# A one-core decoder block: from the planner's instruction order to an order written as a table

## The chip, the cores and the metric

The kernel runs on one core of one Trainium2 chip. The metric is the device time of one execution in microseconds, as the median of the runs. The core has a tensor engine (PE, with its weight loads shown apart as PEld), a vector engine (DVE), a scalar engine (ACT), GpSimd (POOL) and a sync engine (SP) that issues most transfers. Each of them takes its own instructions strictly in the order in which the program lists them, and waits on semaphores for what the others produce. This document is about nothing but that order.

## What is computed

One layer of a hybrid decoder block on 512 tokens of width 1024, in fp32:

```python
h = h + 0.5 * swiglu(rmsnorm(h, norm_ffn1), w1, w3, w2)          # FFN 1, hidden width 2816
z = rmsnorm(h, norm_mix) @ w_in
q, kc, vc, ksl, vsl, kw, vw, g, u = split(z)
o_nsa = nsa_attention(rope(q), ...)     # compressed + selected + window branches, 8 heads of 64
o_s5  = s5_mixer(u, ...)                # 32 groups of 16 channels, 64 states, a scan over time
h = h + concat([o_nsa, o_s5]) @ w_out
h = h + 0.5 * swiglu(rmsnorm(h, norm_ffn2), ...)                 # FFN 2
gate = sigmoid(rmsnorm(h, norm_ple) @ w_ple_gate)
h = h + gate * (p @ w_ple)
return rmsnorm(h, norm_final)
```

## The kernel before

**Number format.** Most products are made of three tensor-engine products (`mm3`, line 157, with `mm` at line 131): each operand is split into a high part and a low part in the fp32r format, and high x high, high x low and low x high are added up in PSUM. A unit of 128x1024 weights comes in by one transfer (`load_unit`, line 103, tile `raw`), ACT casts it to `hi` (line 152), DVE subtracts to get `lo` (line 154). Plain fp32 operands are used only in small products: the S5 scan, the compression branch (`raw` against `cs`, `cosr`, `sinr`), the S5 output gate (`yt`), the row sums of the norms (`ones`) and transposes against `ident`.

**Stages, in order.** FFN 1 in four chunks (`ffn`, line 345; from block 7 of 22 on with a scheme of seven half products, `up_fast`, line 403, whose weights are summed by two accumulating transfers from POOL, lines 362 and 368), with the constants of the S5 scan computed beside it (`s5_constants`). Then the mixer: projections with rotation (`proj`, `rotary`, `kq`), the S5 input `u8`, the S5 scan in eight chunks (`s5_in`, line 904: a product with `si` into bank C, four DVE steps, four scans, one multiply that gives `z`; `s5_out`: products with `so` into bank D; `s5_back`: transposes of `ysb`, copied to `yt`), the scores of four query blocks (`scores`, line 1136: two products and a mask into bank B or C, a row maximum on DVE at line 1169, an exponential on ACT at line 863), the compression branch (`cmp_all`), the S5 output gate (`glu`: two ACT and two DVE steps on each of four `yt`, lines 864 to 871, then products with `yt`), the attention values (`values`, line 1233: products into bank C, two exponentials `e` and `eh`, a subtraction `el` on DVE at line 1264, two products with `VL` into bank D) and the output projection in two halves (`out_half`, the first half is meant to fill gaps between the values). Then a norm, FFN 2, the gate in two column halves, the last norm and the output.

**What sets the order.** The source issues 8,878 instructions and tile-pool marks in the order of its Python loops. The tile framework then takes them and plans, with a model of the durations, an order for each engine in which it keeps data dependencies and the reuse of buffers. The source holds it back in some places: `keep_in_program_order` (called `pinned`) and `issue_after` (in `split`, `combine`, `aside`, `late`, `act`) say that one instruction may not come before another. Weight loads are issued by SP while `more` is set (inside both FFNs) and otherwise by ACT (line 141).

The prediction speaks of source positions: the place of an instruction in that list of 8,878, counted from 0. Those used are

| position | instruction |
|---|---|
| 3543 to 3546 | first S5 product with `si`, chunk 0 |
| 3547 / 4268 | first DVE step of S5 chunk 0 / last DVE step on the fourth `yt` |
| 3887, 3888 | casts of `QA`, `QB` for the second four heads of query block 2 (lines 1149, 1150) |
| 3605 to 3703 | first six exponentials of the scores of query block 3 (line 863) |
| 4160, 4267 | copy of the fourth `yt` out of PSUM (line 947), its Tanh (line 863) |
| 4314 | first product with `yt` |
| 2069, 2088 | cast of `ah` (line 370) and copy of `zx` into bank B (line 399) of one block of FFN 1 |

## Time and profile before

| | us |
|---|---|
| median of 3 runs | 1095.88 |
| lowest, highest | 1093.8, 1096.82 |
| the profiled execution's own time | 1096.0 |
| its span, first to last instruction | 1094.2 |
| PE busy | 1042.1 |
| DVE busy | 794.0 |
| ACT busy | 516.8 |
| POOL busy | 92.7 |

The profile's busy time of PE is a union of matmul records whose ends are modelled, so that a matmul record is longer than the time to the next matmul. Where matmuls run without waiting, the time per matmul is read from the chain that ended last: a run of so many matmuls in so many microseconds. PEclk is the share of the tensor engine's full clock that was granted.

### The profile page before, as it was taken

Reading aid. Unit: us, or ns where it says so; the run is one execution under the profiler, and the core shown is the slowest. Engines: PE = TensorE matmul, PEld = TensorE weight load, DVE = VectorE, ACT = ScalarE, POOL = GpSimd, SP = SyncE. Lnnn points to the kernel's source line nnn. Section 1 sums busy time; section 2 is a strip of 40 time slices with the busy share of each in tenths; the row PEclk is TensorE's granted clock in tenths of the full one; section 3 lists DMA queues with packets and bytes.
Section 4 is the critical chain, followed back from the end, with each engine's and each line's share of the span. In section 5 each row is a group of like instructions: output and inputs, shape, how many; then the busy total and the mean of one; then the engine's idle time right before and its main releaser. Section 6 shows DMA issues by size and latency. Waiting matters only on the chain.

```text
span 1094.2 us, 16835 instructions
## 1 busy us (share of the span) xinstructions
PE 1042.1 (95%) x6446; PEld 897.5 (82%) x6446; DVE 794.0 (73%) x1339; ACT 516.8 (47%) x911; POOL 92.7 (8%) x118
## 2 busy tenths in 40 slices
PE   6999999998999999979799999999999999999996
PEld 4887999798889788767377668799899899898895
DVE  6999786786787766777468887976477557566766
ACT  5334255344435423346647875555255245255541
POOL 5000010000000200010000001011010101000000
PEclk9999999999999999989899999999999999999998
DMA  9334366786657737773621026256365635535302
GB/s 284 137 99 112 81 166 171 192 200 153 166 130 187 234 97 226 216 218 111 187 68 40 0 97 173 77 146 176 84 144 142 177 73 143 171 96 153 111 8 77
DMA packets 86625, 151.14 MB, mean 138 GB/s; under 512 B 27648, under 2 KB 47104, under 8 KB 86544
## 3 DMA queue, kind: packets, MB, share of 16 engines
q1 hardware_dynamic: 66352, 98.11, 29.5%
q0 software_dynamic: 13152, 29.66, 13.7%
q10 hardware_dynamic: 7040, 22.29, 6.5%
q8 instruction: 50, 0.82, 0.3%
q14 instruction: 31, 0.25, 0.1%
HBM read 123.27 MB, written 17.83 MB: 129 GB/s over the span
## 4 chain that ended last, share of the span: by engine, by line
PE 62%; ACT 4%; issue 3%; DVE 3%; DMA 3%; ACTq 0%; SPq 0%; POOLq 0%; POOL 0%; DVEq 0%
PE ps_A L131 18%; PE ps_C L131 18%; PE ps_B L131 17%; PE ps_D L131 10%; DMA qf<-qd 2%; ACT e L863 1%; ACT eh L863 1%; ACT ps_B L863 1%; DMA raw<-in_wpack 1%; DVE el L1264 0%; DVE lo L154 0%; ACT hi L152 0%; DMA qd<-r 0%; ACT QA L1149 0%; ACT pt L1270 0%
## 5 line engine op out<-in xcount | busy, mean ns | idle before, releaser
L152 ACT CAST hi<-raw 128x1024 fp32r<-128x1024 f32 (+2 forms) x201 | 206.0, 1041 | 245.8 <-PE ps_C L131 103.5
L154 DVE TENSOR_TENSOR lo<-raw,hi 128x1024 fp32r<-128x1024 f32 (+2 forms) x201 | 240.0, 1218 | 70.8 <-ACT hi L152 66.4
L131 PE MATMUL ps_C<-hq,hi 128*128 128x512 f32 x704 | 218.0, 392 | 3.9 <-ACT hq L352 2.3
L131 PEld LDWEIGHTS ps_C<-hq,hi 128*128 128x128 f32 x704 | 130.4, 188 | 32.9 <-ACT hq L352 3.2
L131 PE MATMUL ps_A<-xh,hi 128*128 128x256 f32 (+1 forms) x456 | 141.0, 311 | 7.4 <-ACT xh L175 6.3
L131 PE MATMUL ps_A<-xl,hi 128*128 128x256 f32 (+1 forms) x456 | 141.2, 312 | 3.1 <-DVE xl L176 2.1
L131 PE MATMUL ps_A<-xh,lo 128*128 128x256 f32 (+1 forms) x456 | 140.9, 310 | 1.7 <-DVE lo L154 1.7
L131 PE MATMUL ps_C<-hq,lo 128*128 128x512 f32 x352 | 136.2, 390 | 0.0
L131 PEld LDWEIGHTS ps_A<-xh,hi 128*128 128x128 f32 x456 | 86.4, 190 | 12.7 <-ACT xh L175 6.2
L131 PEld LDWEIGHTS ps_A<-xl,hi 128*128 128x128 f32 x456 | 86.2, 190 | 11.6 <-DVE xl L176 4.7
L131 PEld LDWEIGHTS ps_A<-xh,lo 128*128 128x128 f32 x456 | 86.4, 190 | 6.2 <-DVE lo L154 1.9
L131 PE MATMUL ps_B<-sh,hi 128*128 128x256 f32 x280 | 79.1, 283 | 2.7 <-ACT ps_B L399 2.7
L131 PE MATMUL ps_B<-sh,lo 128*128 128x256 f32 x280 | 78.8, 281 | 0.7 <-DVE lo L154 0.7
L131 PE MATMUL ps_B<-sl,hi 128*128 128x256 f32 x280 | 78.9, 282 | 0.0
L131 PEld LDWEIGHTS ps_C<-hq,lo 128*128 128x128 f32 x352 | 66.1, 188 | 13.6
L362 POOL DMA_DIRECT2D raw<-in_wpack x35 | 30.4, 869 | 483.7 <-DVE h L1127 168.3
L488 DVE SCALAR_TENSOR_TENSOR h<-ps_C,h 128x512 f32<-128x512 f32 x64 | 43.9, 689 | 36.8 <-PE ps_C L131 36.4
L131 PE MATMUL ps_D<-sh,hi 128*128 128x256 f32 x220 | 61.7, 283 | 0.4 <-ACT hi L152 0.4
L131 PE MATMUL ps_D<-sh,lo 128*128 128x256 f32 x220 | 61.7, 281 | 0.0
L131 PE MATMUL ps_D<-sl,hi 128*128 128x256 f32 x220 | 61.3, 281 | 0.0
L131 PE MATMUL ps_B<-xh,hi 128*128 128x512 f32 (+1 forms) x164 | 57.9, 353 | 0.9 <-ACT hi L152 0.9
L131 PE MATMUL ps_B<-xh,lo 128*128 128x512 f32 (+1 forms) x160 | 56.0, 350 | 0.8 <-DVE lo L154 0.8
(402 smaller groups left out, 2327.4 us busy)
## 6 DMA issues: line engine op xcount, KB each, us to landing
raw<-in_wpack SPq DMA_DIRECT2D x132, 512.0 KB, 4.3
raw<-in_wpack ACTq DMA_DIRECT2D x40, 512.0 KB, 4.2
raw<-in_wpack POOLq DMA_DIRECT2D x35, 256.0 KB, 4.2
raw<-raw POOLq DMA_DIRECT2D x35, 256.0 KB, 3.4
so<-s5o POOLq DMA_DIRECT2D x8, 768.0 KB, 5.9
si<-s5i POOLq DMA_DIRECT2D x8, 512.0 KB, 5.6
h<-in_xT SPq DMA_DIRECT2D x8, 256.0 KB, 5.5
s5i<-fs SPq DMA_DIRECT2D x4, 512.0 KB, 4.6
```

Of the source, the lines that this page charges most:

```text
L131: return PE.matmul(o, lhsT, rhs, start=start, stop=stop, **kw)
L152: S.copy(hi[:, c], raw[:, c])
L154: V.tensor_tensor(lo[:, c], raw[:, c], hi[:, c].bitcast(F32), OP.subtract)
L362: nc.gpsimd.dma_start(a0[:, 1], src[:, 0:512], accum_op=OP.add)
L488: mark = V.scalar_tensor_tensor(h[:, m, :], o, 0.5, h[:, m, :], OP.mult, OP.add)
L863: S.activation(*args, **kw)
```

## The change

It takes all the holds out (`pinned`, `issue_after`, `aside`'s mark, `late`, `act` and the table of the activation set) and lets every weight load be issued by SP (43 loads of the mixer, of the row embedding and of the gate go from ACT's queue to SP's). No arithmetic, no tile and no loop is changed. In their place stand two tables and a function that is called when the source has issued everything:

```diff
-            load_unit(i, q or (nc.sync if more else nc.scalar))
+            load_unit(i, nc.sync)
...
-                with tc.issue_after(self.last.ins):
-                    for i in range(2):
-                        V.tensor_tensor(t[:, 2 * i:2 * i + 2], a(i), b(i), op)
+                for i in range(2):
+                    V.tensor_tensor(t[:, 2 * i:2 * i + 2], a(i), b(i), op)
...
-        def act(*args, **kw):
-            with tc.issue_after(table[0].ins):
-                S.activation(*args, **kw)
...
-        table.append(tc.keep_in_program_order(S.preload_act_table_set("exp_and_others")))
+        S.preload_act_table_set("exp_and_others")
...
+ENGINE_ORDER = {
+    "PE": (
+        "65:42 31:3 -34:3 3:4 -7:3 28:12 -27 26:30 23:6 -29:3 26:42 26:45 15:3 -18:3 15:18 3:3 -6:3 3:21 65:18 "
...
+    "DVE": (
+        "611 -2 -582 11 -15 -3 5 11 -9 -3 5 -3 26 70 263 232 -233 -264 263:4 6 -7 6 -7:5 2:2 -298 297:7 -303 309 "
...
+    "ACT": (
+        "4 46 -24 11 -15 -3 24 -20 17 -7 -11 1 1 1 14 9 -9 1 1 74 -74 74 64 2 -76 2 54 87 -86 87 -17 -8 79 -70 "
...
+    "SP": (
+        "8 -4 1 -2 2 2 -3:2 1:3 184 193:2 2 -3:2 390:2 -774 770 -585 587 -6 3 -6 -512 2 56 2 109 2 83 2 114 27 "
...
+TILE_ORDER = (
+    "51>792 395>1091 604>948 2341>2356 3185>3260 3186>3261 3227>4160 3281>3594 3468>3731 3532>3556 3533>3562 "
...
+def impose(tc):
+    traced = list(tc.nc.cur_bb.bb.instructions)
+    follow = mybir.DependencyInfo(mybir.DependencyClass.NoSync, mybir.DependencyReason.DATA)
+    for moves in ENGINE_ORDER.values():
+        at, before = 0, None
+        for move in moves.split():
+            step, _, count = move.partition(":")
+            at += int(step)
+            for _ in range(int(count or 1)):
+                if before is not None:
+                    tc.add_manual_dep(traced[at], before.name, follow, reason="order")
+                before = traced[at]
+                at += 1
+    for pair in TILE_ORDER.split():
+        a, b = map(int, pair.split(">"))
+        tc.add_manual_dep(traced[b], traced[a].name, follow, reason="order of tiles")
...
         block_kernel(tc, aps, out)
+        impose(tc)
```

An entry `65:42` says: go 65 places on in the source's list and take 42 instructions in a row; the next entry's step counts from the place behind them, and may be negative. Read in this way the tables name every instruction of its engine once: 6,202 products for PE, 1,339 instructions for DVE, 850 for ACT (843 operations and 7 transfers), 114 for POOL and 333 transfers for SP. Each is made to follow the one in front of it on its engine, so the planner is left no choice. TILE_ORDER's 50 pairs say which of two instructions that share a buffer comes first.

Set side by side with the planner's order, about a third of PE's instructions stand elsewhere relative to the rest (1,996 of 6,202 are outside the longest common sequence; 557 of DVE's 1,339 and 309 of ACT's 850). The large moves are in the mixer:

- The first S5 product (position 3543) comes 123 products later on PE: the 48 products of the compression branch's projections, 51 of the value projection's and eight score groups of three go ahead of it.
- The scores' exponentials 3605 to 3703 come before the casts 3887 and 3888 on ACT; before, they stood behind them.
- All 16 products with `yt` stand in one run; the S5 gate's ACT steps stand close behind the copies of `yt`.
- Of the 192 products of `out_half`'s two calls (96 in each), 15 stand ahead of the first product with `VL`, 48 between the first and the last of them and 129 behind; before it was 96, 2 and 94.
- Neighbours on PE of which one is plain fp32 and the other is not: 93 places, 119 before.

In FFN 1, FFN 2 and the gate the order differs by swaps of groups of three (one `mm3`) between neighbouring runs.

## The prediction

> **What bounds the kernel now.** I read the page first, then the busy time by stretches, then who waited for whom, then the chain of waits around the longest waits. The page:

> ```profile
> PE 1042.1 (95%) x6446; PEld 897.5 (82%) x6446; DVE 794.0 (73%) x1339; ACT 516.8 (47%) x911; POOL 92.7 (8%) x118
> PE 62%; ACT 4%; issue 3%; DVE 3%; DMA 3%; ACTq 0%; SPq 0%; POOLq 0%; POOL 0%; DVEq 0%
> ```

> The tensor engine carries the chain. An order can win only where PE waits or runs slowly, so I ask in which stretches that is. Stretches of the run, with PE's, DVE's and ACT's busy time and PE's granted clock:

> ```profile
> 0.00:25.00 25.00, 15.66 (x59) 10.98 (x60) 16.92 (x15) 15.42 (x23) 13.35 (x16) 1.00 0.90 281
> ...
> 240.00:300.00 60.00, 55.60 (x386) 51.83 (x386) 42.48 (x73) 25.83 (x44) 6.96 (x8) 0.97 0.68 170
> 300.00:440.00 140.00, 137.81 (x764) 119.15 (x763) 99.40 (x154) 55.35 (x80) 12.49 (x22) 1.00 0.62 175
> ...
> 440.00:480.00 40.00, 32.78 (x220) 26.13 (x219) 30.67 (x66) 13.90 (x29) 3.81 (x7) 0.89 0.82 239
> 520.00:560.00 40.00, 33.06 (x155) 18.63 (x152) 19.55 (x35) 22.60 (x48) 0.00 (x0) 0.87 0.47 146
> 552.10:648.20 96.10, 92.37 (x459) 66.90 (x458) 80.41 (x170) 70.92 (x175) 0.00 (x0) 1.00 0.13 39
> 700.00:1000.00 300.00, 300.00 (x2122) 281.95 (x2121) 192.15 (x249) 136.74 (x220) 32.02 (x37) 1.00 0.51 131
> 1000.00:1060.00 60.00, 55.90 (x355) 49.46 (x354) 43.58 (x76) 29.24 (x47) 1.04 (x1) 1.00 0.28 89
> ```

> FFN 2 (700 to 1000) has nothing to give: PE is busy in 300.00 of 300.00 us. PE is idle 4.4 us in 240 to 300 and 2.2 in 300 to 440 (FFN 1), 7.2 in 440 to 480 and 6.9 in 520 to 560 (mixer), 3.7 in the attention (552 to 648) and 4.1 around the gate's start. What the longest waits are for:

> ```profile
> PE ps_B L131 <- ACT ps_B L863: 7.4, 4, 5.9
> PE ps_A L131 <- ACT xh L175: 6.3, 1, 6.3
> PE ps_A L131 <- DVE yt L871: 5.8, 1, 5.8
> PE ps_B L131 <- ACT ps_B L399: 2.7, 1, 2.7
> ```

> The second is the head of the kernel, before any data is there. The other three are mine to explain.

> **The wait for the scores (5.87 us).** The chain and ACT's timeline there:

> ```profile
> 461.45 11.19 DMA qf<-qd
> ...
> 474.15 1.35 PE ps_B L131 x3
> ```

> ```profile
> 472.67 0.63 ACT L1149 ACTIVATE QA<-qf 128x512 fp32r<-128x512 f32 x1 [0.65 <-DMA qf<-qd]
> 473.32 0.66 ACT L863 ACTIVATE ps_B<-ps_B,nmax 128x512 f32<-128x512 f32 x1
> ```

> PE's timeline of the same three products later on:

> ```profile
> 493.51 0.39 PE L131 MATMUL ps_B<-KA,QA 128*128 128x512 f32 x1
> ...
> 494.01 0.37 PE L131 MATMUL ps_A<-hi,xl 128*128 128x280 f32 x1
> ```

> The casts of query block 2 (positions 3888 and 3887) stand on ACT ahead of an exponential that has nothing to do with them. They wait for a transfer of 11.19 us, the exponential waits behind them, and PE waits for the bank that the exponential frees. In the table the first six exponentials of block 3 stand ahead of both casts, so this wait goes. So does the slow stretch behind it: three products took 1.35 us where the same three take 0.50 (493.51 to 494.01). Gain 5.87 + 0.85 = 6.7. What is late next is the exponentials themselves, with two buffers of bank B; I count that below.

> **The wait for the fourth yt (5.84 us).** ACT, DVE and PE:

> ```profile
> 524.32 0.58 ACT L947 COPY yt<-ps_D 128x512 f32<-128x512 f32 x1 [0.30 <-PE ps_D L942]
> ...
> 529.70 0.61 ACT L863 ACTIVATE gt<-yt 128x512 f32<-128x512 f32 x1
> ...
> 536.13 0.61 ACT L863 ACTIVATE gt<-gt 128x512 f32<-128x512 f32 x1
> ```

> ```profile
> 537.73 2.08 PE L131 MATMUL ps_A<-yt,raw 128*128 128x512 f32 x2 [5.84 <-DVE yt L871]
> ```

> ```profile
> 540.23 8.07 PE ps_A L131 x16
> ...
> 549.01 3.20 PE ps_A L131 x7
> ```

> Between the copy and the Tanh ACT does casts that are needed later: 11.8 us for a chain of four steps of about 0.6 us. In the table ten ACT instructions, some 6 us, lie between copy and Tanh, and PE has as cover the compression branch's last products, 32 small score products, two score groups and the first three products with yt (two records each, 0.46 us a record by the last row: 3.20 / 7): about 7 us. The chain is about 9 with its DVE steps and hops, so about 2 us of wait stay (an estimate from these rows). Gain: 5.84, and the slow products behind it, 2.08 - 2 x 0.46 = 1.2 for the first and 8.07 - 16 x 0.46 = 0.7 for the next: 7.7 less 2, so 5.7; I write 6.

> Here the clock enters. The row is this: after a wait of only 2.7 us at 264 PE is slow for a while.

> ```profile
> 265.08 1.75 PE ps_B L131 x10
> ...
> 278.50 1.19 PE ps_B L131 x10
> ```

> Ten products take 1.75 us in place of 1.19. So by the row the 2 us that stay could cost up to as much again, and the sum would be 1071 in place of 1069. [...]

> **Other waits in the mixer.** 7.2 + 6.9 us idle less the two waits leaves 2.4; I take 1.5 off, with 0 and 2.4 as bounds.

> **Plain fp32 products in runs.** A change of kind costs a product's start:

> ```profile
> 494.74 0.29 PE L131 MATMUL ps_A<-lo,xh 128*128 128x280 f32 x1
> 494.87 0.29 PE L131 MATMUL ps_A<-hi,xl 128*128 128x280 f32 x1
> 495.09 0.44 PE L131 MATMUL ps_D<-so,u 128*64 128x128 f32 x4
> 495.46 0.40 PE L131 MATMUL ps_A<-hi,xh 128*128 128x280 f32 x1
> 495.69 0.78 PE L131 MATMUL ps_C<-u,si 128*128 128x64 f32 x6
> ```

> 0.13 us from one to the next of a kind, 0.22 and 0.23 into plain fp32: 0.1 a change. The table has 93 changes, 119 before: 26 x 0.1 = 2.6 (bounds 0 and 5, if one costs 0.2).

> **Attention.** Before, half of out_half's products ran ahead of the values and next to none between them; the stretch's second half is then full on the other engines:

> ```profile
> 560.00:600.00 40.00, 39.20 (x214) 31.23 (x213) 32.85 (x66) 26.10 (x76) 0.00 (x0) 1.00 0.18 53
> 600.00:640.00 40.00, 38.17 (x166) 25.21 (x165) 36.18 (x81) 35.63 (x81) 0.00 (x0) 1.00 0.04 14
> ```

> PE looks busy in both, but runs 166 products in the second where it runs 214 in the first. The table starts the values earlier and puts 48 of those products between them, so that ACT's 70.92 us of the whole 96.10 are spread. If ACT got to 79% of the stretch in place of 74, it would be 90 long: gain 6. Bounds: 10 (ACT at 82%) and -3 (129 products now stand behind the last value, which nobody needs to cover).

> **FFN 1.** 4.4 + 2.2 idle, and the slow products. The wait at 264 has its cause on ACT: the cast of ah (2069) waits for an accumulating transfer and the copy that PE needs (2088) stands behind it. In the table it still does, so I take only part: 4, bounds 7 and -4 (swaps of threes make new waits like it).

> **What I cost at nothing.** Head: the table casts a later slice first (four ACT steps of 0.6 to 0.7 us more ahead of the first product, 1.5 us), and the five waits of 0.7 us for single slices go; 0, within 1.5. FFN 2 can only lose: 0, bound 6. The norm and the gate's start: row sums now stand right behind the last product of FFN 2 and wait for them, but the later wait for the norm goes; 0, within 2. The 43 loads:

> ```profile
> raw<-in_wpack SPq DMA_DIRECT2D x132, 512.0 KB, 4.3
> raw<-in_wpack ACTq DMA_DIRECT2D x40, 512.0 KB, 4.2
> ```

> ```profile
> 513.30 0.33 ACTq L111 DMA_DIRECT2D raw<-in_wpack  x1
> ```

> They land as fast from either queue, and 43 x 0.33 = 14 us of issuing leave ACT where ACT is not last; 0. On SP they now stand in line with the copies of q, k, kc and u, which wait for their producers, and every later load waits with them: bound 4. The end is as it was: the last row sums, the eight multiplies and the output have nothing beside them.

> **The sum.** 6.7 + 6 + 1.5 + 2.6 + 6 + 4 = 26.8 off the profiled execution's 1096.0 (span 1094.2) gives 1069.2; the median of the runs shown, 1095.88, is 0.1 below that execution, so 1069.

> **The rivals.**

> *The waits nearly all go.* All best bounds: 6.7 + 7.7 + 2.4 + 5 + 10 + 7 + 3.5 (head and gate) = 42.3, so 1054. For it: every order is fixed, and only real dependencies are left. Against it: ah still stands ahead of the copy.

> *DVE becomes the bound of the S5 scan.* In the planner's order S5 begins at 439.7; in the table 123 products, about 22 us, go first. DVE then has, from position 3547 to 4268, 129 instructions, which sum to 59.1 us by their own durations; before it had 149, which sum to 75.8:

> ```profile
> 442.70:538.00 95.30, 81.14 (x583) 59.49 (x582) 69.44 (x151) 51.47 (x122) 5.91 (x11) 0.92 0.63 190
> ```

> Busy time is 69.44 as records overlap, so the new stretch has 59.1 x 69.44 / 75.8 = 54 us. My terms for the mixer need it in about 63, DVE at 86%; it has 73% here, and 36.18 of 40 us (90%) only in the attention, where it has no chain of scans to wait through. At 73% it takes 74 and the sum is 1080. At 50%, as in 520 to 560, it takes 108, 45 more than I count, and the sum is 1114. It decides the sign below 58%: then the stretch is 93 us and all 27 are gone.

> *The waits only move.* Each in-order queue gets a new instruction to wait behind, and only the fp32 runs stay: 1093, no change to speak of. For it: 2069 and 2088 keep their order. Against it: the two 6 us waits have causes that the table removes by name. That the table does not do what its name says isn't so on its face, but it is small: 93 changes of kind of 119 are left.

> **How the numbers follow.** The forecast has 0.55, with a range of its own of 1060 to 1081 (1080 is the scan at 73%). All waits gone: 0.22. Waits move: 0.10, of which 0.06 end within 0.3% (3.3 us, about what a measurement of this kernel can tell from no change) and 0.04 just faster. DVE bound and slower: 0.13. So faster 0.55 + 0.22 + 0.04 = 0.81, same 0.06, slower 0.13. Leaving out the slower case and what lies under 1050, the range is 1050 to 1094.

> **What would show it.** In the changed profile: no wait of PE for ACT line 863 over 2 us; a wait for DVE yt of about 2; ACT busy evenly through the attention; DVE at 80 to 90% from the first S5 product to the last yt; 300 us of FFN 2 still 300. Wrong if the S5 stretch is as long as before with DVE under 70%, if FFN 2 shows waits for raw transfers, or if the 264 wait appears in every block of FFN 1.

## The result and the profile after

The changed kernel takes 1079.4 us (median of 4 runs, 1077.9 to 1081.7) against 1096.35 for the kernel before: 0.984 of its time (95% interval 0.981 to 0.988), 17 us less. The forecast was 1069, with a range of 1050 to 1094. The profiled execution is the slowest of the four (1081.65, span 1079.9), so its trace accounts for 14.4 of the 17 us.

The page of the changed kernel: busy time by engine, and the chain that ended last.

```profile
PE 1042.9 (97%) x6446; PEld 902.7 (84%) x6446; DVE 808.2 (75%) x1339; ACT 521.9 (48%) x911; POOL 94.8 (9%) x118
PE 46%; issue 3%; DVE 2%; ACT 2%; POOLq 0%; POOL 0%; DVEq 0%; DMA 0%; SPq 0%; ACTq 0%
```

The 3% that DMA had in the chain are gone (the shares don't add up to 100 on either page, so PE's are not compared). Stretches of the changed kernel (columns as before: PE, PEld, DVE, ACT, POOL busy, PE's clock, DMA share, GB/s): part of FFN 1; first S5 product to first product with yt; the attention from the first to the last product with VL, in two halves; FFN 2; the gate's start.

```profile
240.00:300.00 60.00, 59.73 (x430) 54.95 (x430) 47.50 (x78) 30.22 (x50) 6.96 (x8) 1.00 0.68 169
461.70:523.20 61.50, 58.28 (x519) 45.95 (x518) 54.68 (x132) 38.73 (x101) 5.94 (x11) 0.94 0.61 206
545.90:581.00 35.10, 35.06 (x197) 27.51 (x196) 29.93 (x53) 31.31 (x92) 0.00 (x0) 1.00 0.05 16
581.00:616.80 35.80, 35.59 (x151) 24.05 (x149) 32.02 (x72) 31.72 (x65) 0.00 (x0) 1.00 0.00 1
690.00:990.00 300.00, 297.67 (x2071) 276.16 (x2070) 188.49 (x240) 134.21 (x215) 30.37 (x35) 1.00 0.51 133
1011.20:1024.00 12.80, 9.82 (x52) 8.63 (x51) 8.23 (x17) 6.51 (x8) 1.95 (x1) 0.73 0.38 103
```

In the S5 scan DVE is busy 89% and PE waits little; in the attention ACT is at 89% in both halves. But FFN 2, 300.00 of 300 before, now idles 2.3 us, and the gate's start, 12.8 us behind the last product of FFN 2, runs 52 products at a clock of 0.73. The same stretch of the kernel before:

```profile
1029.10:1042.00 12.90, 11.22 (x95) 10.95 (x94) 11.43 (x18) 8.50 (x10) 1.04 (x1) 1.00 0.60 185
```

What PE waits for in the changed kernel (total, times, longest):

```profile
PE ps_A L130 <- ACT xh L173: 7.7, 1, 7.7
PE ps_D L130 <- DVE dg L322: 3.4, 3, 2.1
PE ps_A L130 <- DVE xl L174: 2.7, 2, 1.7
PE ps_D L130 <- DVE acc L184: 2.5, 2, 2.2
PE ps_B L130 <- DVE t L418: 2.2, 1, 2.2
...
PE ps_B L130 <- ACT ps_B L1152: 0.3, 2, 0.2
```

The scores' wait (7.4 us in four) is 0.3; the wait for yt is no longer there. New are the row sums (acc) and a wait of 2.2 in FFN 1, at 351.

To set stage against stage I use PE's losses: the length of a stretch less what its products would take at the spacing from start to start that is usual for their form. It takes in the waits and the slow products alike. Worked out for the profiled executions, us:

| stretch | before | after | e1 | e9 |
|---|---|---|---|---|
| up to the first product | 6.3 | 7.7 | 8.2 | 8.0 |
| FFN 1 | 19.1 | 16.4 | 14.1 | 15.9 |
| mixer, to the last product with yt | 29.5 | 13.5 | 12.5 | 13.4 |
| attention and out_half | 12.6 | 7.0 | 7.0 | 7.0 |
| norm | 0.0 | 1.8 | 2.5 | 1.8 |
| FFN 2 | 5.8 | 8.9 | 5.5 | 3.4 |
| gate | 7.3 | 10.9 | 7.4 | 7.3 |
| behind the last product | 7.3 | 7.3 | 7.3 | 7.3 |

Before less after is 14.4 in all: 24.3 won in FFN 1, the mixer and the attention, 1.4 lost at the head, and 8.5 given back in the norm, FFN 2 and the gate. Executions with the same order differ too: in eight profiles FFN 1 by the table loses 13.6 to 16.4 us, in three by the planner (before, e4 and e11) 18.4 to 19.1. So a difference of 2 or 3 us there between two columns says little by itself.

### The profile page after: what moved, and what is told of

It is laid out like the page before. It is cut to its first block, busy times and chain, and to the rows that moved or that the text cites. A ratio compares the mean times of both kernels' runs of the same rounds, so it can differ in the third digit from the quotient of the medians.

```text
span 1079.9 us, 16852 instructions
## 1 busy us (share of the span) xinstructions
PE 1042.9 (97%) x6446; PEld 902.7 (84%) x6446; DVE 808.2 (75%) x1339; ACT 521.9 (48%) x911; POOL 94.8 (9%) x118
## 3 DMA queue, kind: packets, MB, share of 16 engines
q0 software_dynamic: 13152, 29.66, 13.5%
## 4 chain that ended last, share of the span: by engine, by line
PE 46%; issue 3%; DVE 2%; ACT 2%; POOLq 0%; POOL 0%; DVEq 0%; DMA 0%; SPq 0%; ACTq 0%
PE ps_C L130 13%; PE ps_A L130 13%; PE ps_B L130 12%; PE ps_D L130 8%; ACT hi L151 1%; DVE lo L152 0%; ACT pu L375 0%; DVE ple L1430 0%; DVE h L1107 0%; DVE h L478 0%; DVE acc L184 0%; ACT sq L183 0%; ACT eh L1242 0%; ACT e L1238 0%; DVE dg L322 0%
## 5 line engine op out<-in xcount | busy, mean ns | idle before, releaser
L151 ACT CAST hi<-raw 128x1024 fp32r<-128x1024 f32 (+2 forms) x201 | 208.7, 1042 | 260.2 <-PE ps_C L130 116.6
L152 DVE TENSOR_TENSOR lo<-raw,hi 128x1024 fp32r<-128x1024 f32 (+2 forms) x201 | 245.4, 1228 | 78.7 <-ACT hi L151 76.2
L130 PEld LDWEIGHTS ps_B<-sh,hi 128*128 128x128 f32 x280 | 52.7, 188 | 6.7 <-ACT pu L375 5.4
## 6 DMA issues: line engine op xcount, KB each, us to landing
raw<-in_wpack SPq DMA_DIRECT2D x172, 512.0 KB, 4.3
si<-s5i POOLq DMA_DIRECT2D x8, 512.0 KB, 7.7
s5i<-fs SPq DMA_DIRECT2D x4, 512.0 KB, 5.8
s5o<-gt SPq DMA_DIRECT2D x4, 512.0 KB, 4.7
```

Source lines behind the costliest of these rows:

```text
L130: return PE.matmul(o, lhsT, rhs, start=start, stop=stop, **kw)
L151: S.copy(hi[:, c], raw[:, c])
L152: V.tensor_tensor(lo[:, c], raw[:, c], hi[:, c].bitcast(F32), OP.subtract)
```

## The experiments

Ten kernels are the changed kernel with another table: for some source positions the entries are the planner's. Where two orders meet, they are merged by the time at which each would issue an instruction, so that near the junction some come later than in either. Pairs of TILE_ORDER with a replaced position are left out. Each ratio is to the kernel before, run beside it. The fences on the edits say in short what was changed, not in the kernel's own text.

**e1: the planner's order from FFN 2 on.**

```diff
 positions    0 to 5357: table
-positions 5358 to 8877: table
+positions 5358 to 8877: planner's order
```

> The table is kept through FFN 1, the mixer, the attention and the norm before FFN 2; from the first product of FFN 2 on every engine has the planner's order, written as a table. Theory 1 (the changed order of FFN 2 and of the gate loses what the forecast missed: PE loses 8.9 us in FFN 2 after and 5.8 before, 10.9 and 7.3 from its last product to the last row sum): 1079.4 less 6.6 is 1073, ratio 0.979. Rival A (those losses are no matter of the order, but come with whatever else is new, the loads on SP or an earlier arrival): 1079, ratio 0.984. Rival B (the profiled execution is 2 to 3 us worse there by chance): 1076 to 1079.

Measured: 1072.5 us, 0.979 (0.976 to 0.981). Theory 1 gave 1073. FFN 2 and the gate lose 5.5 and 7.4 us, as in the kernel before. The table from FFN 2 on, two fifths of the positions, is better left out (the changed kernel's interval, 0.981 to 0.988, only touches this one; e9 below is clear of it).

**e2: the table in the mixer alone.**

```diff
-positions 0 to 3160 and 5358 to 8877: table
+positions 0 to 3160 and 5358 to 8877: planner's order
```

> The planner's order in FFN 1, FFN 2 and the gate, the table's in the mixer, the attention and the norm, all loads on SP. Theory 1 (only the mixer and the attention gain, 16.0 and 5.6 us of PE's losses, less 1.8 in the norm): 1096.4 less 19.8 is 1076.6, ratio 0.982. Rival A (FFN 2 and the gate lose with any order once the mixer is done sooner): 1096.4 less 13.2 is 1083, ratio 0.988. If FFN 1's order also matters, as forecast with 4: 2 to 4 above e1.

Measured: 1089.05 us, 0.994 (0.992 to 0.996), 12 above theory 1 and above both rivals. The mixer loses 25.7 us where it loses 13.5 in the table. Waits of PE in this kernel:

```profile
PE ps_A L130 <- ACT xh L173: 10.4, 3, 6.8
PE ps_D L130 <- DVE dg L322: 5.9, 3, 2.9
```

The first is the head's one wait (6.8) and two more, of 3.1 and 0.4 us, at the junction: the table's first projection meets the planner's last casts of FFN 1. From the last product of FFN 1 to the first S5 product this kernel loses 12.5 us where the changed kernel loses 0.8, which is nearly all of the difference. The junction is what was measured; e11 puts it elsewhere.

**e3: the planner's order in the mixer alone.**

```diff
-positions 3161 to 5357: table
+positions 3161 to 5357: planner's order
```

> The table in FFN 1, FFN 2 and the gate, the planner's order in the mixer, the attention and the norm, all loads on SP. Theory 1: 1079.4 plus 19.8 is 1099, ratio 1.003, so the table without its mixer is no faster, or a little slower, than the kernel before. Rival (the gain is spread over the kernel): 1085 to 1090, ratio 0.99 to 0.995.

Measured: 1102.0 us, 1.006 (1.004 to 1.008). Without its mixer the table is slower than the kernel before, as theory 1 says and more so: FFN 2 behind this junction loses 14.2 us, 5.3 more than in the changed kernel. But the mixer itself loses some 27 us again and the attention 13, much as before the change. The gain is not spread over the kernel.

**e4: the planner's order everywhere, loads on SP.**

```diff
-positions 0 to 8877: table
+positions 0 to 8877: planner's order, with the 43 loads on SP
```

> The planner's order of the kernel before on every engine, written as a table, with no hold and with the 43 loads on SP as the only difference. The forecast priced the loads at 0 with a bound of +4: 1096, ratio 1.000. Rival (14 us of issuing taken off ACT are part of the gain): 1088 to 1093. Rival (loads stand behind copies on SP that wait): up to 1100, ratio 1.004.

Measured: 1096.25 us, 0.999 (0.998 to 1.001). The 43 loads on SP and the missing holds cost and bring nothing, within 3 us.

**e5: the casts ahead of the exponentials again.**

```diff
 ACT: 3605 3625
+     3890 3888 3887
      3630 3649 3654 3703
-     3890 3888
      3708 3915 3736 4011
-     3887
```

> The table with one place changed: on ACT the copy 3890 and the casts 3888 and 3887 of query block 2 stand again where the planner had them, behind the second of the six exponentials and ahead of the third (3630). Theory (the forecast's cause of the scores' wait): in the profile of after their transfers are issued at 454.8 and 455.5 us and land some 4 us later, the copy and the two casts take 1.0 and 1.2 us, so the third exponential, at 456.8 in after, starts near 460.6; PE waits about 4 us for ACT's exponential, with about 0.9 us of slow products behind it: 1079.4 plus 4.7 is 1084, ratio 0.989. Rival (PE's other products or the early start of the transfers cover it): 1079 to 1080, ratio 0.985, no wait over 1 us.

Position 3890 is a copy that goes with the two casts. The planner, too, had the first two of the six exponentials (3605 and 3625) ahead of the casts, and not all six behind them as the section on the change says. Measured: 1086.85 us, 0.989 (0.987 to 0.991), 5.3 us above the changed kernel by the ratios; theory 1084, ratio 0.989. ACT's timeline and PE's wait:

```profile
461.56 0.63 ACT L1130 ACTIVATE QB<-qf 64x512 fp32r<-64x512 f32 x1 [2.24 <-DMA qf<-qd]
462.10 0.61 ACT L1129 ACTIVATE QA<-qf 128x512 fp32r<-128x512 f32 x1
462.62 0.63 ACT L1152 ACTIVATE ps_B<-ps_B,nmax 128x512 f32<-128x512 f32 x1
```

```profile
PE ps_B L130 <- ACT ps_B L1152: 3.6, 2, 3.5
```

The cast waits for its transfer, the exponential behind it for the cast, PE for the exponential: three instructions in the wrong place make the wait again. The mixer's losses go from 13.5 to 19.2.

**e6: the planner's order in the attention.**

```diff
-positions 4388 to 5242: table
+positions 4388 to 5242: planner's order
```

> The table up to the products with yt, the planner's order for the attention values, out_half and the products of the row embedding beside them (96 products of out_half ahead of the first product with VL, 2 between, 94 behind), the table again from the norm on. Theory (48 products of out_half between the values are what the attention gained): 1079.4 plus 5.6 is 1085, ratio 0.990, PE's losses between the last product with yt and the last of out_half 12.6 us in place of 7.0. Rival (the attention gains only because the scores ahead of it are further on): 1079 to 1081, ratio 0.985.

Measured: 1093.4 us, 0.996 (0.994 to 0.997), more than either. The attention itself does what the theory says, 12.8 us of losses in place of 7.0, and comes near its old length of 96.1 us, with ACT at 75% as before (columns as above; last product with yt to last with VL; the changed kernel takes 78.5):

```profile
538.90:632.60 93.70, 90.00 (x428) 64.39 (x426) 74.26 (x143) 69.86 (x172) 0.00 (x0) 1.00 0.11 34
```

The rest lies at the junctions: 3.3 us more net in front of and between the products with yt (two of them now wait 1.8 and 2.3 us), 4.1 in the norm.

**e7: the planner's order from the gate on.**

```diff
-positions 8293 to 8877: table
+positions 8293 to 8877: planner's order
```

> The table up to the end of FFN 2, the planner's order from the gate on: the four row sums stand 26 products behind the last product of FFN 2 in place of right behind it. Theory (e1 split: the row sums' wait of 2.2 us, the cast's lo that DVE queues behind the sums' ms, and the slow products behind that wait cost 3.6 us): 1079.4 less 3.6 is 1075.8, ratio 0.981, and the rest of e1's gain, 3.3 us, is FFN 2's. Rival (FFN 2's order alone carries e1): 1079, ratio 0.984.

Measured: 1079.58 us, 0.983 (0.981 to 0.986): the rival's number. The losses of the gate stay at 10.7. PE no longer waits for the row sums, but as long in the same place for a cast of weights:

```profile
PE ps_A L130 <- ACT hi L151: 2.4, 1, 2.4
```

So the row sums' place alone is not the price: the gate's casts must come earlier too, and they belong to FFN 2's end. e10 takes that in.

**e10: the planner's order from FFN 2's last sum on.**

```diff
-positions 7918 to 8877: table
+positions 7918 to 8877: planner's order
```

> The table up to position 7918, the start of FFN 2's last sum of down products, and the planner's order from there through the gate, with a junction at which no instruction had to be moved. Theory (e7 failed because its junction put the cast of the gate's first weights late on ACT, not because the gate's start costs nothing): the gate's losses fall from 10.9 to 7.3 us: 1079.4 less 3.6 is 1075.8, ratio 0.981. Rival (the gate's start is bound by the casts in any order, and e1's gain is FFN 2's): 1078 to 1079, ratio 0.984.

Measured: 1076.52 us, 0.980 (0.978 to 0.982); theory 1075.8. The gate's start in this kernel, again from the last product of FFN 2 on:

```profile
1010.30:1023.10 12.80, 11.12 (x94) 10.86 (x93) 11.32 (x18) 8.31 (x10) 1.97 (x1) 1.00 0.50 165
```

94 products in the time of 52, at a clock of 1.00. PE still waits 1.7 us there, for DVE's lo, but no slow products follow. The losses of the gate are 7.9. The rival's 0.984 lies outside the interval.

**e11: the planner's order in FFN 1.**

```diff
-positions 0 to 3060: table
+positions 0 to 3060: planner's order
```

> The planner's order from the start to the last products of FFN 1 (position 3061), the table from there. It is e2 with the other junction and the table's FFN 2 and gate. Theory (FFN 1's order is worth what PE's losses say, 19.1 and 18.4 us by the planner against 13.6 to 16.4 by the table, less 1.4 to 1.9 for the table's later first product): 1 to 3 above after, 1079.4 plus 2 is 1081.5, ratio 0.986. Rival (e2's 16 us above e1 belong to FFN 1's order itself and not to its junction): 1090 or more, ratio 0.994.

Measured: 1083.27 us, 0.987 (0.985 to 0.989); theory 1081.5. The interval overlaps that of the changed kernel. FFN 1 loses 18.7, the head 6.9, the mixer 13.6: the mixer's gain does not need FFN 1's table, and e2's failure was its junction.

**e9: the table first, the planner's order behind it.**

```diff
-positions 5929 to 8877: table
+positions 5929 to 8877: planner's order
```

> The table up to a product of FFN 2's third block (position 5929) at which both orders have issued the same products, the planner's order from there to the end, so that the junction does not fall on the norm as in e1. Theory: e1's 1072.5 less what e1 lost at its junction (waits of 1.4 and 0.9 us behind the first products of FFN 2 and 0.6 in the norm): 1070, ratio 0.976. Rival (the junction costs nothing net, what e1 won is all there is): 1072 to 1073, ratio 0.979.

Measured: 1070.9 us, 0.975 (0.973 to 0.977), the fastest kernel here; theory 0.976. e1 was not run beside it, and their intervals overlap, so the gain over e1 is not shown. FFN 2 in it:

```profile
690.00:990.00 300.00, 298.52 (x2092) 278.82 (x2092) 189.36 (x245) 136.13 (x219) 30.38 (x35) 1.00 0.54 139
```

**e8: kinds and waits by themselves.** Only products on constant operands. In the fences of e8 and e12 `fr(n)` stands for n products in fp32r (of 256 columns, or of the second number), `f32(n)` for n in plain fp32, `so(n)` and `si(n)` for n plain fp32 products of the shapes of the S5 scan, and `wait(n)` for a wait of PE.

```diff
+fr(96); f32(96)                              # runs
+48 x: fr(1); f32(1)                          # turns of one, then of four, of eight
+wait(n); fr(60), wait(n); fr(64), ...        # n + 2 ACT copies between two products
```

> Not the block: only products on constant operands, the output is filled with a constant. First runs of 96 fp32r products of 256 columns and 96 plain fp32 products of 128 (then of 64) columns, then the same numbers in turns of one, of four and of eight; then runs of 60 to 75 fp32r products of 512 columns, each behind a wait of PE of about 1 to 4 us made by a chain of ACT copies, each length four times; then three waits of about 1 us with 2, 6, 12 or 20 products between them. Price of a change of kind: forecast 0.1 us, so turns of one take 96 x 0.1 = 9.6 us longer than the two runs, turns of four 2.4, turns of eight 1.2. Rival: 0, the longer spacing belongs to the shapes and not to the change. [...]

PE's timeline (start, length, product, count; a plain fp32 product leaves two records): the run of 96 plain fp32 products, and turns of one.

```profile
30.88 21.60 PE L41 MATMUL ps_B<-xf,wf 128*128 128x128 f32 x192
52.24 0.36 PE L37 MATMUL ps_A<-xr,wr 128*128 128x256 f32 x1
52.44 0.38 PE L41 MATMUL ps_B<-xf,wf 128*128 128x128 f32 x2
52.58 0.36 PE L37 MATMUL ps_A<-xr,wr 128*128 128x256 f32 x1
```

A pair takes 0.34 us (52.24 to 52.58). In runs it takes 0.120 (11.51 for 96) and 0.222 (21.36), which is 0.342. Going into plain fp32 a product starts 0.20 behind the other in place of 0.12, but the way back gives it back. Turns of one, four and eight take 32.6, 32.8 and 32.9 us per 96 and 96, the runs 32.9: a change of kind costs nothing on the full array.

The waits (in brackets) and the runs of products behind them:

```profile
363.30 0.30 PE L37 MATMUL ps_A<-z,wr 128*128 128x64 f32 x1 [1.68 <-ACT z L52]
363.44 15.90 PE L37 MATMUL ps_A<-xr,wr 128*128 128x512 f32 x69
...
437.25 0.30 PE L37 MATMUL ps_A<-z,wr 128*128 128x64 f32 x1 [2.23 <-ACT z L52]
437.38 17.54 PE L37 MATMUL ps_A<-xr,wr 128*128 128x512 f32 x69
...
457.18 0.30 PE L37 MATMUL ps_A<-z,wr 128*128 128x64 f32 x1 [2.23 <-ACT z L52]
457.31 17.29 PE L37 MATMUL ps_A<-xr,wr 128*128 128x512 f32 x75
```

69 products take 15.90 us behind 1.68, 17.54 behind 2.23; 75 behind another 2.23 take 17.29, no loss. Where there is a loss, seven or more of the products stand 0.43 us apart in place of 0.23.

**e12: half-array products.**

```diff
+so(96); fr(72, 280)                          # runs
+24 x: so(4); fr(3, 280)                      # turns of 4, then of 12, of 24
+si(64); fr(48, 280)
+16 x: si(4); fr(3, 280)                      # turns of 4, then of 16
+wait(5); fr(60, 512), ...                    # 24 runs of 60 to 74, n 5, 6 and 7
```

> Not the block: only products on constant operands, the output is filled with a constant. e8 had no product of the S5 scan's own shapes. Here the plain fp32 products with so (half the array's columns, 128 columns each) and those with si (64 columns) stand first in runs of 96 and 64 beside runs of 72 and 48 fp32r products of 280 columns, then in turns of 4, 12 and 24 (si: 4 and 16). If runs of the scan's shapes are worth something, the turns of 4 take 24 x 2 x 0.1 = 4.8 us longer than the two runs by the forecast's price, the turns of 24 0.8; if not, 0 as in e8. [...]

The timeline: runs of so and of fp32r, two turns of 4, and turns of 12; then si.

```profile
19.05 10.70 PE L49 MATMUL ps_B<-xf,u 128*64 128x128 f32 x192
29.68 9.48 PE L38 MATMUL ps_A<-xr,wr 128*128 128x280 f32 x72
39.09 0.66 PE L49 MATMUL ps_B<-xf,u 128*64 128x128 f32 x8
39.68 0.65 PE L38 MATMUL ps_A<-xr,wr 128*128 128x280 f32 x3
40.26 0.66 PE L49 MATMUL ps_B<-xf,u 128*64 128x128 f32 x8
...
86.65 1.53 PE L49 MATMUL ps_B<-xf,u 128*64 128x128 f32 x24
88.11 1.42 PE L38 MATMUL ps_A<-xr,wr 128*128 128x280 f32 x9
89.46 2.84 PE L49 MATMUL ps_B<-xf,u 128*64 128x128 f32 x48
```

A turn of 4 and 3 takes 1.17 us (39.09 to 40.26); by the runs it would take 4 x 0.111 + 3 x 0.131 = 0.84. A turn of 12 and 9 takes 2.81 against 2.51. So two changes between so and fp32r cost 0.3 us, about 0.15 each; summed over the sections, turns of 4, 12 and 24 take 27.9, 22.5 and 21.0 us against 20.0 for the runs, or 0.16, 0.15 and 0.12 a change. With si, turns of 4 and 16 take 20.4, the runs 20.4. What costs is not the number format: so uses half of the array's columns (128*64 in its rows), si and fp32r all of them. The rows give the price and not its cause: so's products also lie on the two halves of the columns by turns, and take 0.111 us each in a run, where a plain fp32 product on the full array takes 0.222 (e8).

## Why the prediction was right, point by point

- **Scores' wait (6.7).** Right: 0.3 us of waits are left, and e5 brings 5.3 us back by the two casts and the copy alone.
- **Fourth yt (6, 2 us of wait to stay).** Not right in kind, and its size was not measured alone. No product with yt waits any more, so the 2 us did not come. But the work in front of these products now waits four times, 2.8 us in all (0.81, 0.85, 0.47, 0.65):

```profile
512.16 0.44 PE L130 MATMUL ps_D<-so,u 128*64 128x128 f32 x4 [0.81 <-DMA so<-s5o]
...
514.54 0.71 PE L922 MATMUL ps_D<-ident,ysb 64*128 64x64 f32 x8 [0.85 <-ACT ysb L917]
...
516.09 0.44 PE L130 MATMUL ps_D<-w,chid 128*31 128x64 f32 x4 [0.47 <-ACT yt L927]
...
517.18 0.39 PE L130 MATMUL ps_B<-KAc,QA 128*128 128x64 f32 x1 [0.65 <-DVE KAc L1068]
```

  The granted clock is 0.50 from 516.34 to 526.58: a pair of the 32 small score products takes 0.29 us (517.18 to 517.47), where it takes 0.16 at 1.00 in the kernel before (554.64 to 554.80). So the cover lasts 7 us, as the forecast had it. The chain of yt (515.46 to 523.05) takes 7.6 where the forecast had about 9. At 0.16 a pair these products alone would be 2.1 us shorter and some wait would have been left (an estimate from these times); that none was left is in part luck. No run undid this step alone. With the scores' wait, the others (1.5) and the runs, the mixer was to gain 16.8 and gained 16.0; only the sum is confirmed.
- **Plain fp32 in runs (2.6).** The size was about right, the reason wrong. The step that failed: "0.13 us from one to the next of a kind, 0.22 and 0.23 into plain fp32: 0.1 a change." e8 shows that this is given back at the other end. What the table can save are changes to and from products on part of the array: the 96 products with so stand in 8 runs of 12, by the planner in 19 runs of 1 to 12, and the part of the array in use (128*128, 128*64 and so on in the rows) changes 53 times in place of 76: 23 x 0.15 = 3.5 us. That is an estimate by e12's price, which was measured for so's shape only; no run of the block undid the runs alone.
- **Attention (6).** Right in size and cause: 5.6, and e6 loses 5.8 with the old order. ACT came to 89% in both halves, as forecast evenly. The sum behind it was not right, and there luck helped: the stretch to the last product with VL is 78.5 us at 87% of ACT (68.05 of 78.50), where the forecast had 90 at 79%, but the products that stand behind it, priced only in the lower bound, take 30.1 us to the last of out_half in place of 21.5.
- **FFN 1 (4, with the head at 0).** 2.7 in this execution, and 2 to 5.5 over all of them (above); the head lost 1.4, within its 1.5 (with the same head 3.3 in the profile of e5). e11, which gives both back, is 3.9 us slower than the changed kernel by the medians, 2.5 by the ratios, with intervals that overlap. The wait at 264, which the forecast let stand because the cast of ah still goes ahead of the copy, is gone; the one at 351 is new.
- **The 43 loads (0).** Right, with the planner's order: e4.
- **DVE as the bound of the S5 scan.** It did not decide: 54.68 of 61.5 us, where the forecast had 54 of 63. (By the forecast's own figures the 27 us are gone at a stretch of 90 us, DVE at 60%, and not at 93 and 58%.)
- **FFN 2 (0, bound 6), the gate's start and the norm (0, within 2 each).** Here is most of the 10 us that did not come: the first lost 3.1 us, the second 3.6, the norm 1.8. In FFN 2 the weight loads wait for ACT's copy pu nine times, and the one shown sets PE back by 0.3 us (0.39 from start to start, 792.47 to 792.86, in place of 0.12). With the planner's order in FFN 2 there is no such wait (the kernel before, e1, e9), so it comes with the table's order there. The changed kernel, 662 to 1011:

```profile
PEld ps_B L130 <- ACT pu L375: 3.0, 9, 0.4
```

```profile
792.86 0.19 PEld L130 LDWEIGHTS ps_B<-sh,hi 128*128 128x128 f32 x1 [0.32 <-ACT pu L375]
```

  At the gate the step that failed is "row sums now stand right behind the last product of FFN 2 and wait for them, but the later wait for the norm goes". That wait was seen and cost at nothing net, without what queues behind it: DVE takes ms, which needs the sums, ahead of lo, which PE's next products need, and these run slowly, at a granted clock of 0.50 from 1014.69 to 1021.52.

```profile
1013.80 1.08 PE L130 MATMUL ps_D<-ones,acc 128*128 128x1 f32 x8 [2.23 <-DVE acc L184]
...
1015.00 1.22 DVE L152 TENSOR_TENSOR lo<-raw,hi 128x1024 fp32r<-128x1024 f32 x1
...
1016.27 0.58 PE L130 MATMUL ps_A<-xh,lo 128*128 128x256 f32 x1 [0.75 <-DVE lo L152]
...
1016.65 0.41 PE L130 MATMUL ps_A<-xh,hi 128*128 128x256 f32 x1
1016.86 0.41 PE L130 MATMUL ps_A<-xl,hi 128*128 128x256 f32 x1
```

  The last two start 0.21 us apart; from 1022.42 on, at a clock of 1.00, it is 0.12. e10 takes this back; in e7 the place of the sums alone did not.
- **The clock.** The sum takes 0 for slow products behind the 2 us of wait at yt (1069; with them 1071). No run shows that such a wait always goes without them: behind 1.96 us 5 of 8 waits were followed by slow products, behind 2.23 us 7 of 12 (e8 and e12, below). The wait of 2 us at yt did not come, but those of 2.2 us at 351 and at the gate were followed by a granted clock of 0.50 (352.50 to 355.91, 1014.69 to 1021.52), and so were the short waits in front of yt (516.34 to 526.58).
- **The rivals.** That all waits go was too much: new ones came in FFN 2, the gate and the norm. That waits only move is what happened there, and there alone.

## What to carry to other kernels

Price an order stage by stage: where PE is busy 300 of 300 us, leave the order as it is: here the new one only lost there. It is the ends of such a stage that have something to give: of the 5.8 us that the kernel before loses in FFN 2, some 4.5 fall in the first 12 us and the last 23, and e9, with the table at the start of FFN 2 and the planner's order behind, loses 3.4. When a step is moved next to what it waits for, price what queues behind it on the other engines and what PE's clock does behind the wait, not the wait alone. Read a price of changing over from both ends of a turn, or from whole turns against whole runs.

## What the runs showed of the hardware

```profile
397.90:401.31 3.41, 1.18 (x7) 0.87 (x6) 0.00 (x0) 1.92 (x8) 0.00 (x0) 1.00 0.00 0
401.31:404.72 3.41, 3.41 (x10) 2.63 (x9) 0.00 (x0) 0.00 (x0) 0.00 (x0) 0.50 0.02 5
...
452.51:455.92 3.41, 2.44 (x12) 1.86 (x10) 0.00 (x0) 0.84 (x4) 0.00 (x0) 1.00 0.00 0
455.92:459.33 3.41, 2.15 (x10) 1.81 (x11) 0.00 (x0) 1.08 (x5) 0.00 (x0) 1.00 0.00 0
```

- **The half clock came behind less idle time, too.** In the changed kernel's mixer the clock halved at 516.34, behind a stretch of 3.41 us in which PE was idle only 1.3 us (2.10 busy of 3.41, with the waits of 0.85 and 0.47 us in it) and ran small products on part of the array. Three waits of 0.58 us, with 2 to 20 products of 256 columns on the full array between them, were not followed by slow products (e8). What set the clock at 516.34 is not shown.
- **Half-array products.** A change between so (128*64) and fp32r on the full array cost 0.12 to 0.16 us in e12. Between plain fp32 and fp32r on the full array turns took no longer than runs: 32.6 to 32.9 us against 32.9 in e8, 20.4 against 20.4 with si in e12.
